# A hybrid decoder step on one core: the second layer's normalised operand is multiplied out ahead of the K/V evacuations, and the sample queries' copies are issued on ScalarE

## The chip, the cores and the metric

The kernel runs on one core of one Trainium2 chip. The metric is the device time of one execution in microseconds (us). The kernel before takes 1169.92 us, the median of three runs (1169.79 to 1174.06). Engines are named as in the profile: PE is TensorE, DVE VectorE, ACT ScalarE, POOL GpSimd, SP SyncE, which issues the DMAs.

## The reference

One step of a two-layer decoder of width 1024 runs on 512 prompt tokens and on 8 samples of 8 tokens each, 576 tokens in all. Layer 1 is a gated linear recurrence (HGRN2). Then one shared K/V is projected from its output, and layer 2 is sliding-window attention with a learned sink per head, over that K/V and, for the samples, over cached rows:

```python
hp, sp = hgrn2_layer(hp, s_zero, w_in_a, w_out_a, norm_a, onorm_a, lb)     # prompt
hs, ss = hgrn2_layer(hs, state_hgrn, w_in_a, w_out_a, norm_a, onorm_a, lb) # samples
kv_p, kv_s = shared_kv(hp, norm_kv, w_kv), shared_kv(hs, norm_kv, w_kv)    # rms_norm(x, g) @ w
q, gate = split(rms_norm(x, norm_b) @ w_in_b)
s = where(window_mask, q @ k.T * 64 ** -0.5, -inf)
p = softmax(concatenate([s, sink]))[..., :-1]
x = x + ((p @ v) * silu(gate)) @ w_out_b
y = rms_norm(x, norm_f)
```

Layer 2 has 32 query heads of 64 columns in 4 groups, each with one K/V head. The window is 128 tokens. All is float32.

## The kernel before

**Arithmetic.** Every float32 operand of a large product is split in two fp32r tiles: hi is a cast, lo is what the cast lost. A product is three passes over the contraction, w_hi·x_hi, w_hi·x_lo, w_lo·x_hi (`product_cols`, matmuls on L211). The weights come by DMA as "raw" and are split in `split_weights`: hi by ACT's cast (L200), lo by a subtraction (L204). Which engine subtracts is set by `share`: during the K/V projection DVE takes a quarter and POOL three quarters, in layer 2 POOL takes all (1024 columns in one instruction).

**Stages.** Layer 1 goes on to about 690 us, the K/V projection from there to about 718 us, its turning and the first queries to about 742, the attention to about 1142, the output projection's end, the final norm and the stores to the end. Tokens are worked on as columns, in two halves j of HN = 288. The hidden state is `hT` (128 partitions x 8 tiles k x 576), the normalised operand that the products read is `xhi`, `xlo` of the same shape.

**The layer boundary.** The K/V projection is run in two pairs of products: c0 = 0 makes K, c0 = 2 makes V. It reads the hidden state times its own norm's gain from `xhi`, `xlo`, made at the end of layer 1; each product `pkv` is 24 matmuls of 288 columns into a bank of PSUM, evacuated by DVE into `kf` with the factor 1/rms (the tile `rall`, `rts[j]` in the code; L1030). For K, ACT casts `KDh` (L1048), DVE subtracts `KDl` (L1051). For V, PE transposes `kf` into `pvw` (L1062), from which `Vc` is taken. Only when the V products of a half j have been computed may `xhi`, `xlo` of that half be overwritten with layer 2's operand. That is what `scaled` does (L515 to 521), for each k of a half: DVE multiplies `hT` by the gain and 1/rms into a tile u (288 columns, tag "nu", four buffers; L519), ACT casts it to `xhi` (L520), and POOL for even k, DVE for odd k subtracts into `xlo` (L521). With four buffers, the product for k + 4 waits until u of k has been subtracted.

**Layer 2.** `queries` makes the queries of two heads at a time: a product into a bank `pbq`, from which ACT casts QS (L1286), DVE subtracts into the other half of QS (L1289) and, where the bank holds the 64 sample tokens' queries too (j = 1), DVE copies these into `Qs` in two instructions of 64 columns (L1294). `attend_sample` runs the samples' scores `scs` on `Qs` (L1205, 1206). The prompt's attention goes through scores, softmax (`P`), transposition (`ph`, `pl`, `pk`), the product with V (`pav`, `low`) and the gate into `sgt`; `split_out` splits sgt into `ohb` (ACT, L1394) and `olb` (DVE, L1395), `sample_part` does the same for the samples' 64 columns (`ohb` L1266, `olb` L1267), and `out_halves` runs the output product `po` on them, added to hT on L1334. All these tiles lie in the pool `ab`; in it P, ph, pl and sgt have two buffers each.

**What sets the order.** The parts of layer 2 are interleaved by a written order and a pace per step (`ORDER`, `PACE`), and the tile scheduler then orders each engine's instructions by priority: code under `tc.high_priority(offset=BOOST)` (800) or `early(EARLYB)` (100) is put that far ahead of its place in the program. Each engine then executes its list in order. A tile that is read and written by several engines is guarded by semaphores. PSUM banks for the products are in rotation: three for `pkv`, `pbq`, `pbg` and `po` together, five for the rest.

Of the kernel before, what the change touches and what calls it, by code (L numbers as in the profile page):

```python
# [10 lines left out]
F32 = mybir.dt.float32  # L11
# [5 lines left out]
ALU = mybir.AluOpType  # L17
PSUM = bass.MemoryType.PSUM

P = 128  # L20
D = 1024
KT = D // P
# [5 lines left out]
HN = T // 2  # L28
# [55 lines left out]
def yoco_kernel(  # L84
# [26 lines left out]
    act, dve, pool, pe, sp = nc.scalar, nc.vector, nc.gpsimd, nc.tensor, nc.sync  # L111
# [20 lines left out]
    def half(name):  # L132
        return ps["m"].tile([P, 512], F32, tag="m", name=name)
# [50 lines left out]
    def vec(name, i):  # L184
        r, _ = vcol[name]
        return vT[:, r + i : r + i + 1]

    hT = res.tile([P, KT, T], F32, name="hT")
# [6 lines left out]
    def split_weights(src, name, parts=None):  # L195
        n = src.shape[1] * src.shape[2]
        raw = wts.tile([P, 1024], F32, tag="raw", name=f"raw_{name}", bufs=3)
        sp.dma_start(raw[:, :n].rearrange("p (a c) -> p a c", a=src.shape[1]), src)
        hi, lo = parts or [wts.tile([P, 1024], F32R, tag=t, name=f"{t}_{name}") for t in ("whi", "wlo")]
        act.copy(hi[:, :n], raw[:, :n])  # L200
        c = n * share[0] // 8
        for eng, r in ((dve, slice(0, c)), (pool, slice(c, n))):
            if r.start < r.stop:
                eng.tensor_tensor(lo[:, r], raw[:, r], hi[:, r].bitcast(F32), ALU.subtract)  # L204
        return hi, lo
# [13 lines left out]
    def product_half(pm, whi, wlo, x, j, width=P, w0=0, nk=KT):  # L219
        product_cols(pm, whi, wlo, x, j * HN, (j + 1) * HN, width, w0, nk)  # L220
# [42 lines left out]
    rts = [rall[:, j * HN : (j + 1) * HN] for j in range(2)]  # L263
# [248 lines left out]
        act.activation(rt, pss[:, :HN], AF.Ln, bias=eps_c, scale=1.0 / D)  # L512
        act.activation(rt, rt, AF.Exp, scale=-0.5)

    def scaled(rt, gname, one, j):  # L515
        r = slice(j * HN, (j + 1) * HN)
        for k in range(KT):
            u = one(f"u_{gname}{k}_{j}")
            dve.scalar_tensor_tensor(u, hT[:, k, r], vec(gname, k), rt, ALU.mult, ALU.mult)  # L519
            act.copy(xhi[:, k, r], u)  # L520
            (dve if k % 2 else pool).tensor_tensor(xlo[:, k, r], u, xhi[:, k, r].bitcast(F32), ALU.subtract)  # L521

# [3 lines left out]
    with ExitStack() as actx:  # L526
# [12 lines left out]
        for i in range(2):  # L539
            t = per.tile([P, T], F32, name=f"Xl{i}")  # L540
            dve.memset(t, 0.0)
            Xs.append(t)
            t = per.tile([P, DB, 16], F32, name=f"Qz{i}")
            dve.memset(t, 0.0)
            Qz.append(t)
            t = per.tile([P, P], F32, name=f"atts{i}")
            dve.memset(t, 0.0)
            att_s.append(t)
            t = per.tile([P, P], F32, name=f"vs{i}")
# [407 lines left out]
        for h in range(NH):  # L957
            nxt, chunks, n = {}, [], 0
# [21 lines left out]
    with ExitStack() as bctx:  # L980
# [33 lines left out]
        ab = bctx.enter_context(tc.tile_pool(name="ab", bufs=1))  # L1014
        with tc.tile_pool(name="kvx", bufs=1) as kvx:
            kvo = kvx.tile([P, 512], F32, name="kvo")
            kvs = kvx.tile([LS, 512], F32, name="kvs")
            kvw = [w_kv[:, c * P : (c + 1) * P].rearrange("(k p) c -> p k c", p=P) for c in range(4)]
            kfs = []
            for c0 in range(0, 4, 2):  # L1020
                ws = [split_weights(kvw[c], f"kv{c}") for c in (c0, c0 + 1)]
                kf = [kvx.tile([P, T], F32, tag=f"kf{c % 2}", name=f"kf{c}", bufs=2) for c in (c0, c0 + 1)]
                for j in range(2):
                    for c in range(2):
                        pm = half(f"pkv{c0 + c}_{j}")
                        product_half(pm, *ws[c], bx, j)
                        if c0 == 0 and c == 0:
                            with tc.high_priority(offset=BOOST):
                                feature_norm(j)
                        dve.tensor_tensor(kf[c][:, j * HN : (j + 1) * HN], pm[:, :HN], rts[j], ALU.mult)  # L1030
                    if c0:
                        with tc.high_priority(offset=BOOST):
                            scaled(
                                rts[j],
                                "norm_b",
                                lambda n: kvx.tile([P, HN], F32, tag="nu", name=n, bufs=4),
                                j,
                            )
                kfs += kf
            for c in range(4):  # L1040
                kf = kfs[c]
                if c < 2:
                    for gi in range(2):
                        g = 2 * c + gi
                        r0 = slice(64 * gi, 64 * gi + 64)
                        for s in range(2):
                            o0 = slice(64 * s, 64 * s + 64)
                            act.copy(KDh[o0, g, :], kf[r0, :LP])  # L1048
                        same, other = r0, slice(64 - 64 * gi, 128 - 64 * gi)
                        for o0 in (same, other):  # L1050
                            dve.tensor_tensor(KDl[o0, g, :], kf[r0, :LP], KDh[r0, g, :].bitcast(F32), ALU.subtract)  # L1051
                    act.copy(kS[:, c, :], kf[:, LP:])
                    pt = misc(f"pkw{c}")
                    pe.transpose(pt[:, :P], kf[:, LP - P : LP], ident)
                    pe.transpose(pt[:LS, P : 2 * P], kf[:, LP:], ident)
                    dve.tensor_copy(kvo[:, c * P : (c + 1) * P], pt[:, :P])
                    dve.tensor_copy(kvs[:, c * P : (c + 1) * P], pt[:LS, P : 2 * P])
                else:
                    g0 = 2 * (c - 2)
                    pt = misc(f"pvw{c}")  # L1060
                    for n in range(NC):
                        pe.transpose(pt[:, n * P : (n + 1) * P], kf[:, n * P : (n + 1) * P], ident)  # L1062
                    pt4 = pt.rearrange("p (n g d) -> p n g d", n=NC, g=2)
                    hi = Vc[:, :, g0 : g0 + 2, :64]
                    act.copy(hi, pt4)
                    dve.tensor_tensor(Vc[:, :, g0 : g0 + 2, 64:], pt4, hi.bitcast(F32), ALU.subtract)
                    dve.tensor_copy(kvo[:, c * P : (c + 1) * P], pt[:, 3 * P :])
                    pt2 = misc(f"pvs{c}")
                    pe.transpose(pt2[:LS, :P], kf[:, LP:], ident)
                    dve.tensor_copy(kvs[:, c * P : (c + 1) * P], pt2[:LS, :P])  # L1070
            dve.tensor_copy(vS[:LS, :], kvs[:, 256:])
            sp.dma_start(kvw_prompt[0].rearrange("s k g d -> s (k g d)"), kvo)
            for bb in range(DB):
                sp.dma_start(co[bb, P - DL :, :], kvs[bb * DL : (bb + 1) * DL, :])
# [194 lines left out]
        def queries(i, Qs, QS):  # L1269

            g, pp = i // 2, i % 2
            gr = slice(64 * (g % 2), 64 * (g % 2) + 64)
            hv = [slice(64 * par, 64 * par + 64) for par in range(2)]
            for pr in range(2):
                m = 2 * i + pr
                w = split_weights(w_in_b[0, :, m * P : (m + 1) * P].rearrange("(k p) c -> p k c", p=P), f"bq{m}")
                for j in range(2):
                    pm = half(f"pbq{m}_{j}")
                    c0, c1 = ((0, 256), (256, T))[j]
                    product_cols(pm, *w, bx, c0, c1)  # L1280
                    n = 256
                    Q = QS[pr][:, 4 * j : 4 * j + 4, :].rearrange("p b (a q) -> p a b q", a=2)
                    pq = pm[:, :n].rearrange("p (b q) -> p b q", b=4)
                    with early(EARLYB):
                        for par in range(2):
                            act.copy(Q[hv[par], par, :, :], pq[hv[par]])  # L1286
                        for par in range(2):
                            a, o = hv[par], hv[1 - par]
                            dve.tensor_tensor(  # L1289
                                Q[o, par, :, :], pq[a], Q[a, par, :, :].bitcast(F32), ALU.subtract  # L1290
                            )
                        if j == 1:
                            for par in range(2):
                                dve.tensor_copy(  # L1294
                                    Qs[gr, :, 4 * pp + 2 * pr + par, :],
                                    pm[hv[par], n : n + LS].rearrange("p (b i) -> p b i", i=8),
                                )
                    yield
# [142 lines left out]
        size = list(itertools.accumulate(8 if kind == "O" else 4 for kind, _ in order))  # L1441
# [131 lines left out]
```

## Time and profile before

| | |
|---|---|
| median of 3 runs | 1169.92 us (1169.79 to 1174.06) |
| profiled execution, its own time | 1169.39 us |
| its span in the trace | 1167.6 us |
| mean granted PE clock | 0.982 of full speed |
| PE busy | 1111.7 us, 95% |
| DVE busy | 895.4 us, 77% |
| ACT busy | 702.1 us, 60% |
| POOL busy | 340.7 us, 29% |

The profile is of one execution. Its span runs from the first recorded instruction to the last; the execution's own time is 1.8 us longer. A row of a timeline gives the start of a run of like instructions in us from the span's start, its duration, the engine, the line in the kernel, the operation with output and inputs, and in brackets the idle time of the engine before it with what ended it. Where a row ends in x4, its duration is that of four instructions. Windows give the busy time of each engine in a stretch and the clock that PE was granted there.

### The profile page before, as it was taken

To read this page: it belongs to the slowest core of one execution; us is meant where nothing else is said; L and a number is where in the kernel's file an instruction comes from. 1 tells how busy PE (TensorE), PEld (TensorE's weight loads), DVE (VectorE), ACT (ScalarE), POOL (GpSimd) and SP (SyncE) were. 2 spreads that over 40 slices of the span, in tenths; PEclk is the share of its full clock that TensorE was granted. 3 is DMA by queue.
4 is the path that set the end of the run, shared out by engine and by line. 5 is a ranking of instruction groups with operands and counts; after the bars stand their busy time and mean duration, and the time that the engine had idled before them with its cause. 6 is when DMAs were issued, how large, how long until landed. Compare 5 with 4: busy or idle time off the path is not lost.

```text
span 1167.6 us, 27339 instructions
## 1 busy us (share of the span) xinstructions
PE 1111.7 (95%) x10937; PEld 1078.1 (92%) x10937; DVE 895.4 (77%) x2090; ACT 702.1 (60%) x1700; POOL 340.7 (29%) x311
## 2 busy tenths in 40 slices
PE   5999999999999999999999987999999999999997
PEld 5999999999999999999999987989989999999986
DVE  8898776489984597893897779567787778777686
ACT  6776764466662567772767455557655764765545
POOL 1122221112121131110122155444543453454430
PEclk8999999999999999999999998989999999999999
DMA  5332233232332523332232332211212213112102
GB/s 154 100 112 86 84 109 112 59 110 76 110 117 66 147 74 113 97 107 74 76 111 77 103 91 74 68 55 56 73 39 71 74 55 91 56 55 73 56 19 82
DMA packets 161097, 98.01 MB, mean 84 GB/s; under 512 B 3897, under 2 KB 157546, under 8 KB 160938
## 3 DMA queue, kind: packets, MB, share of 16 engines
q1 hardware_dynamic: 160970, 96.26, 28.0%
q8 instruction: 86, 1.41, 0.5%
q14 instruction: 41, 0.34, 0.1%
HBM read 84.06 MB, written 14.16 MB: 84 GB/s over the span
## 4 chain that ended last, share of the span: by engine, by line
PE 45%; DVE 11%; ACT 6%; issue 2%; POOL 1%; DVEq 0%; ACTq 0%; POOLq 0%
PE pbg L211 7%; PE po L211 7%; PE pbq L211 5%; PE po L228 4%; PE pg L228 3%; PE pf L228 3%; PE pi L228 3%; PE pq L228 2%; PE pkv L211 2%; PE sc L1098 2%; ACT P L1127 1%; PE pav L1181 1%; PE pz L211 1%; DVE QS L1289 1%; PE pa L797 1%
## 5 line engine op out<-in xcount | busy, mean ns | idle before, releaser
L606 POOL TENSOR_TENSOR Xl<-Xl 128x72 f32<-128x72 f32 x80 | 50.3, 659 | 205.9 <-DVE Xl L603 204.7
L638 POOL TENSOR_TENSOR sg<-sg,lg 128x576 f32<-128x576 f32 x16 | 26.3, 1642 | 278.4 <-ACT lg L571 278.4
L200 ACT CAST whi_a<-raw_a 128x1024 fp32r<-128x1024 f32 x64 | 67.1, 1049 | 63.4 <-PE po L228 30.8
L204 DVE TENSOR_TENSOR wlo_a<-raw_a,whi_a 128x1024 fp32r<-128x1024 f32 x64 | 81.8, 1282 | 25.0 <-issue 23.6
L1127 ACT ACTIVATE P<-P,st 128x192 f32<-128x192 f32 (+2 forms) x128 | 54.1, 424 | 68.4 <-DVE st L1122 68.4
L1136 POOL TENSOR_SCALAR P<-P,st 128x192 f32<-128x192 f32 (+1 forms) x64 | 48.6, 769 | 117.9 <-DVE st L1129 99.4
L438 DVE TENSOR_TENSOR hT<-hT,po 128x576 f32<-128x576 f32 x32 | 24.1, 754 | 49.6 <-PE po L228 49.3
L200 ACT CAST whi_o<-raw_o 128x1024 fp32r<-128x1024 f32 x30 | 31.4, 1047 | 30.8 <-PE po L228 25.6
L204 POOL TENSOR_TENSOR wlo_bg<-raw_bg,whi_bg 128x1024 fp32r<-128x1024 f32 x16 | 38.4, 2402 | 35.5 <-ACT whi_bg L200 30.0
L228 PE MATMUL po<-oh,whi_o 128*128 128x288 f32 x256 | 42.8, 302 | 4.4 <-ACT whi_o L200 1.9
L211 PE MATMUL po<-olb,whi_o 128*128 128x288 f32 x224 | 43.0, 306 | 3.8 <-DVE olb L1395 1.9
L211 PE MATMUL po<-ohb,whi_o 128*128 128x288 f32 x224 | 43.6, 311 | 2.4 <-DVE Qs L1294 1.7
L662 POOL TENSOR_TENSOR vb<-vst,bmask 128x512 fp32r<-128x512 f32 x32 | 36.7, 1168 | 26.7 <-DVE vst L658 13.8
L204 POOL TENSOR_TENSOR wlo_bq<-raw_bq,whi_bq 128x1024 fp32r<-128x1024 f32 x16 | 38.8, 2430 | 19.2 <-ACT whi_bq L200 19.1
L228 PEld LDWEIGHTS po<-oh,whi_o 128*128 128x128 f32 x256 | 35.9, 188 | 6.3 <-ACT whi_o L200 2.2
L211 PE MATMUL pbq<-xhi,whi_bq 128*128 128x256 f32 (+1 forms) x256 | 41.4, 305 | 0.0
L211 PE MATMUL po<-ohb,wlo_o 128*128 128x288 f32 x224 | 41.3, 301 | 0.0
L228 PE MATMUL po<-ol,whi_o 128*128 128x288 f32 x256 | 40.5, 294 | 0.0
L211 PE MATMUL pbg<-xhi,whi_bg 128*128 128x288 f32 x256 | 40.5, 300 | 0.0
L228 PE MATMUL po<-oh,wlo_o 128*128 128x288 f32 x256 | 40.4, 294 | 0.0
L211 PE MATMUL pbg<-xhi,wlo_bg 128*128 128x288 f32 x256 | 40.1, 299 | 0.0
L204 POOL TENSOR_TENSOR wlo_o<-raw_o,whi_o 128x1024 fp32r<-128x1024 f32 x14 | 33.6, 2399 | 22.0 <-ACT whi_o L200 20.3
(385 smaller groups left out, 3761.4 us busy)
## 6 DMA issues: line engine op xcount, KB each, us to landing
raw_a<-in_w_in_a_dram SPq DMA_DIRECT2D x64, 512.0 KB
S<-in_state_hgrn_dram SPq DMA_DIRECT2D x32, 256.0 KB
out_dram<-S SPq DMA_DIRECT2D x32, 256.0 KB
raw_o<-in_w_out_a_dram SPq DMA_DIRECT2D x16, 512.0 KB
raw_bq<-in_w_in_b_dram SPq DMA_DIRECT2D x16, 512.0 KB
raw_bg<-in_w_in_b_dram SPq DMA_DIRECT2D x16, 512.0 KB
raw_o<-in_w_out_b_dram SPq DMA_DIRECT2D x16, 512.0 KB
xt<-in_x_prompt_dram SPq DMA_DIRECT2D x4, 512.0 KB
```

Source lines behind the costliest of these rows:

```text
L200: act.copy(hi[:, :n], raw[:, :n])
L204: eng.tensor_tensor(lo[:, r], raw[:, r], hi[:, r].bitcast(F32), ALU.subtract)
L211: pe.matmul(pm[:, : c1 - c0], w[:, k * width + w0 : k * width + w0 + P], x(k)[i][:, c0:c1], start=n == 0, stop=n == len(terms) - 1,)
L228: pe.matmul(pm[:, j, :HN], w[:, k * width + c0 : k * width + c0 + P], x(k, j), start=n == 0 and k == 0, stop=n == 2 and k == nk - 1,)
L438: dve.tensor_add(h2, h2, ps2(pm))
L606: pool.tensor_tensor(X8[:, :, j : j + 1], X8[:, :, j : j + 1], X8[:, :, k : k + 1], ALU.add)
L638: (pool if SGP else dve).tensor_tensor(sg, sg, l, ALU.mult)
L662: pool.tensor_tensor(t, view(vst.bitcast(F32), [[0, 4], [1, P]], off=half * P), view(bmask, [[1, 4], [0, P]]), ALU.mult,)
L797: pe.matmul(pa[32 * j : 32 * j + ns, c, t0 : t0 + nt], keys[:, c * P + s0 : c * P + s0 + ns], queries[:, c * P + t0 : c * P + t0 + nt], st ...
L1098: pe.matmul(sc[:, hf, k0[hf] :], QS[pr][:, 2 * n + hf, :], kk[:, g, ks], start=q == 0, stop=q == 1)
L1127: act.activation(x, x, AF.Exp, bias=st[:, a : a + 1], accum_out=st[:, 8 + a : 9 + a])
L1136: (pool if e == "p" else dve).tensor_scalar(x, x, st[:, 8 + a : 9 + a], None, ALU.mult)
```

## The change

Two things are changed. First, `scaled` makes only the products, into tiles that it is given, and a new function `operand` makes the cast and the subtraction. All 16 products are issued once, after the first pair of K/V products, into tiles that live until the operand is made: four of 288 columns in the old "nu" buffers, the others in the attention's buffers of P (two tiles of two products each), ph and pl (four tiles), and sgt (two tiles, four products). `operand` stands where `scaled` stood, after the second pair's evacuations of a half, with the same offset. Second, the two copies into `Qs` are issued on ACT in place of DVE.

```diff
--- before.py
+++ after.py
@@ -512,11 +512,16 @@
         act.activation(rt, pss[:, :HN], AF.Ln, bias=eps_c, scale=1.0 / D)
         act.activation(rt, rt, AF.Exp, scale=-0.5)
 
-    def scaled(rt, gname, one, j):
+    def scaled(us, gname, j):
+
         r = slice(j * HN, (j + 1) * HN)
-        for k in range(KT):
-            u = one(f"u_{gname}{k}_{j}")
-            dve.scalar_tensor_tensor(u, hT[:, k, r], vec(gname, k), rt, ALU.mult, ALU.mult)
+        for k, u in enumerate(us):
+            dve.scalar_tensor_tensor(u, hT[:, k, r], vec(gname, k), rts[j], ALU.mult, ALU.mult)
+
+    def operand(us, j):
+
+        r = slice(j * HN, (j + 1) * HN)
+        for k, u in enumerate(us):
             act.copy(xhi[:, k, r], u)
             (dve if k % 2 else pool).tensor_tensor(xlo[:, k, r], u, xhi[:, k, r].bitcast(F32), ALU.subtract)
 
@@ -1030,12 +1035,15 @@
                         dve.tensor_tensor(kf[c][:, j * HN : (j + 1) * HN], pm[:, :HN], rts[j], ALU.mult)
                     if c0:
                         with tc.high_priority(offset=BOOST):
-                            scaled(
-                                rts[j],
-                                "norm_b",
-                                lambda n: kvx.tile([P, HN], F32, tag="nu", name=n, bufs=4),
-                                j,
-                            )
+                            operand(us[j], j)
+                if not c0:
+
+                    us = [[kvx.tile([P, HN], F32, tag="nu", name=f"nu{k}", bufs=4) for k in range(4)], []]
+                    for n, (tag, size) in enumerate((("P", 2), ("P", 2), ("ph", 1), ("pl", 1), ("ph", 1), ("pl", 1), ("sgt", 3), ("sgt", 1))):
+                        t = ab.tile([P, size * HN], F32, tag=tag, name=f"us{n}", bufs=2)
+                        us[n > 1] += [t[:, i * HN : (i + 1) * HN] for i in range(size)]
+                    for i in range(2):
+                        scaled(us[i], "norm_b", i)
                 kfs += kf
             for c in range(4):
                 kf = kfs[c]
@@ -1291,7 +1299,7 @@
                             )
                         if j == 1:
                             for par in range(2):
-                                dve.tensor_copy(
+                                act.copy(
                                     Qs[gr, :, 4 * pp + 2 * pr + par, :],
                                     pm[hv[par], n : n + LS].rearrange("p (b i) -> p b i", i=8),
                                 )
```

How DVE's list at the layer boundary changes is shown by its rows from the place on where the first kf is evacuated (names are out<-inputs, the number behind a name is that of the tile, the last column partitions x elements; u_norm_b are the products in the kernel before). Before:

```order
L519 SCALAR_TENSOR_TENSOR u_norm_b_0_9516<-hT,vT,rall 128x288
L519 SCALAR_TENSOR_TENSOR u_norm_b_0_9520<-hT,vT,rall 128x288
L519 SCALAR_TENSOR_TENSOR u_norm_b_0_9524<-hT,vT,rall 128x288
L519 SCALAR_TENSOR_TENSOR u_norm_b_0_9528<-hT,vT,rall 128x288
L1030 TENSOR_TENSOR kf_9334<-pkv_0_9336,rall 128x288
L1030 TENSOR_TENSOR kf_9335<-pkv_0_9366,rall 128x288
L1030 TENSOR_TENSOR kf_9334<-pkv_1_9392,rall 128x288
L204 TENSOR_TENSOR wlo_kv_9451<-raw_kv_9448,whi_kv_9450 128x256
L1051 TENSOR_TENSOR KDl<-kf_9334,KDh 64x512 x3
```

After (nu and us are the products, L1035 and L1059 are the old L1030 and L1051):

```order
L1035 TENSOR_TENSOR kf_9334<-pkv_0_9336,rall 128x288
L519 SCALAR_TENSOR_TENSOR nu_9448<-hT,vT,rall 128x288
L519 SCALAR_TENSOR_TENSOR nu_9449<-hT,vT,rall 128x288
L519 SCALAR_TENSOR_TENSOR nu_9450<-hT,vT,rall 128x288
L519 SCALAR_TENSOR_TENSOR nu_9451<-hT,vT,rall 128x288
L519 SCALAR_TENSOR_TENSOR us_9452<-hT,vT,rall 128x288 x2
L519 SCALAR_TENSOR_TENSOR us_9453<-hT,vT,rall 128x288
L1035 TENSOR_TENSOR kf_9335<-pkv_0_9366,rall 128x288
L519 SCALAR_TENSOR_TENSOR us_9453<-hT,vT,rall 128x288
L519 SCALAR_TENSOR_TENSOR us_9454<-hT,vT,rall 128x288
L519 SCALAR_TENSOR_TENSOR us_9455<-hT,vT,rall 128x288
L519 SCALAR_TENSOR_TENSOR us_9456<-hT,vT,rall 128x288
```

The first evacuation now stands ahead of all products; the products, which stood four ahead of it and twelve behind the K operands, stand between the evacuations of the first pair.

The second place on DVE is the end of the boundary, ahead of the last two evacuations kf, the ones that PE's transposes `pvw` read. Before:

```order
L521 TENSOR_TENSOR xlo<-u_norm_b_0_9536,xhi 128x288
L519 SCALAR_TENSOR_TENSOR u_norm_b_1_9600<-hT,vT,rall 128x288
L519 SCALAR_TENSOR_TENSOR u_norm_b_1_9604<-hT,vT,rall 128x288
L519 SCALAR_TENSOR_TENSOR u_norm_b_1_9608<-hT,vT,rall 128x288
L521 TENSOR_TENSOR xlo<-u_norm_b_0_9544,xhi 128x288
L1030 TENSOR_TENSOR kf_9463<-pkv_0_9490,rall 128x288
L519 SCALAR_TENSOR_TENSOR u_norm_b_1_9612<-hT,vT,rall 128x288
L1030 TENSOR_TENSOR kf_9462<-pkv_1_9548,rall 128x288
L1030 TENSOR_TENSOR kf_9463<-pkv_1_9574,rall 128x288
```

After:

```order
L1035 TENSOR_TENSOR kf_9490<-pkv_0_9492,rall 128x288
L1059 TENSOR_TENSOR KDl<-kf_9335,KDh 64x512 x2
L526 TENSOR_TENSOR xlo<-nu_9449,xhi 128x288
L1035 TENSOR_TENSOR kf_9491<-pkv_0_9518,rall 128x288
L526 TENSOR_TENSOR xlo<-nu_9451,xhi 128x288
L526 TENSOR_TENSOR xlo<-us_9452,xhi 128x288
L526 TENSOR_TENSOR xlo<-us_9453,xhi 128x288
L1035 TENSOR_TENSOR kf_9490<-pkv_1_9560,rall 128x288
L1035 TENSOR_TENSOR kf_9491<-pkv_1_9586,rall 128x288
```

The four products that stood among the subtractions there are gone; four subtractions xlo stand in front of the last two kf where two stood.

On POOL the sequence of operations is the same at this place, and so are the orders on PE and of SP's DMAs. The third place is where a bank of queries with the samples' columns is taken up. DVE before, in the attention's unit whose olb of 64 columns follows:

```order
L1395 TENSOR_TENSOR olb_0_11234<-sgt_10324,ohb_0_11233 128x512
L1395 TENSOR_TENSOR olb_1_11240<-sgt_10324,ohb_1_11239 128x512
L1289 TENSOR_TENSOR QS_1_11046<-pbq_1_11250,QS_1_11046 64x4x64 x2
L1294 COPY Qs_9697<-pbq_1_11250 64x8x8 x2
L1267 TENSOR_TENSOR olb_1_11240<-oS_10816,ohb_1_11239 128x64
L1157 TENSOR_TENSOR pl_0_0_11288<-ptr_0_0_11281,ph_0_0_11287 128x256
L1164 TENSOR_TENSOR pk_0_0_11291<-ptm_0_0_11282,pk_0_0_11291 64x256
```

ACT after, with what each instruction waits for in brackets (the semaphore of an engine or of a DMA queue):

```order
L1402 CAST ohb_0_11229<-sgt_10320 128x512 [waits DVE_49]
L1402 CAST ohb_1_11235<-sgt_10320 128x512
L1274 CAST ohb_1_11235<-oS_10812 128x64
L1294 CAST QS_1_11042<-pbq_1_11246 64x4x64 [waits PE_49]
L1294 CAST QS_1_11042<-pbq_1_11246 64x4x64
L1164 CAST ph_0_0_11283<-ptr_0_0_11277 128x256 [waits PE_49]
L1169 CAST pk_0_0_11287<-ptm_0_0_11278 64x256 [waits PE_49]
L200 CAST whi_o_2_11410<-raw_o_2_11408 128x1024 [waits DMAHW3_49,Pool_49]
L1302 COPY Qs_9693<-pbq_1_11246 64x8x8 [waits DVE_49]
L1302 COPY Qs_9693<-pbq_1_11246 64x8x8
```

The two copies, which stood on DVE between its subtractions into QS and the olb subtraction of 64 columns, stand on ACT behind the casts of QS, ph, pk and a weight cast, and the first of the two waits for DVE.

## The prediction

> **What bounds the kernel now.** The page comes first: its span, its busy times and the chain that ended last.
>
> ```profile
> span 1167.6 us, 27339 instructions
> PE 1111.7 (95%) x10937; PEld 1078.1 (92%) x10937; DVE 895.4 (77%) x2090; ACT 702.1 (60%) x1700; POOL 340.7 (29%) x311
> PE 45%; DVE 11%; ACT 6%; issue 2%; POOL 1%; DVEq 0%; ACTq 0%; POOLq 0%
> ```
>
> TensorE (PE) is busy for 95% of the span. Another engine's saving counts only where PE waits for it, so I read the stretches in which PE waits. First the layer boundary, in the timelines of PE, DVE, POOL and ACT (start, duration, engine, line; in brackets the idle time before and its releaser).
>
> ```profile
> 718.06 0.38 PE L1062 MATMUL pvw<-ident,kf 128*128 128x128 f32 x2
> 724.78 0.69 PE L1062 MATMUL pvw<-ident,kf 128*128 128x128 f32 x2 [6.33 <-DVE kf L1030]
> ```
> ```profile
> 695.68 1.81 DVE L519 SCALAR_TENSOR_TENSOR u_norm_b<-hT,vT,rall 128x288 f32<-128x288 f32 x4 [2.39 <-ACT rall L513]
> 706.18 0.46 DVE L1030 TENSOR_TENSOR kf<-pkv,rall 128x288 f32<-128x288 f32 x1
> 708.31 2.81 DVE L1051 TENSOR_TENSOR KDl<-kf,KDh 64x512 fp32r<-64x512 f32 x4
> 716.30 6.12 DVE L519 SCALAR_TENSOR_TENSOR u_norm_b<-hT,vT,rall 128x288 f32<-128x288 f32 x3
> 724.28 0.81 DVE L1030 TENSOR_TENSOR kf<-pkv,rall 128x288 f32<-128x288 f32 x2
> 727.86 1.06 DVE L521 TENSOR_TENSOR xlo<-u_norm_b,xhi 128x288 fp32r<-128x288 f32 x1
> ```
> ```profile
> 702.01 1.84 POOL L204 TENSOR_TENSOR wlo_kv<-raw_kv,whi_kv 128x768 fp32r<-128x768 f32 x1 [6.85 <-ACT whi_kv L200]
> 717.13 4.98 POOL L204 TENSOR_TENSOR wlo_bq<-raw_bq,whi_bq 128x1024 fp32r<-128x1024 f32 x2
> 727.56 2.01 POOL L521 TENSOR_TENSOR xlo<-u_norm_b,xhi 128x288 fp32r<-128x288 f32 x2 [3.52 <-ACT xhi L520]
> ```
>
> PE runs dry at 718.44 and waits 6.33 us for the last kf evacuations, which stand on DVE behind three products that take 6.12 us; four took 1.81 us at 695.68. The slow three lie under POOL's two L204 subtractions: a DVE instruction with two SBUF inputs does not run while a POOL subtraction runs, and one slips through between two of POOL's. Afterwards the clock is about halved (the windows view; busy us of PE, PEld, DVE, ACT, POOL, then the granted PE clock, DMA share and GB/s; two later places are shown with it):
>
> ```profile
> 724.00:730.00 6.00, 5.22 (x26) 5.15 (x27) 6.00 (x15) 2.93 (x7) 2.05 (x3) 0.54 0.26 77
> 856.00:860.00 4.00, 4.00 (x21) 4.00 (x21) 2.46 (x13) 1.96 (x9) 0.00 (x0) 0.59 0.42 121
> 960.00:964.00 4.00, 2.97 (x14) 3.00 (x15) 3.84 (x10) 1.34 (x4) 2.28 (x1) 0.71 0.14 33
> 964.00:968.00 4.00, 4.00 (x29) 4.00 (x29) 2.43 (x13) 1.92 (x10) 0.00 (x0) 0.87 0.29 102
> ```
>
> Then the attention, 726 to 1142 us, in the view of waits (total, times, longest):
>
> ```profile
> PE scs L1205 <- DVE Qs L1294: 5.0, 2, 2.8
> PE po L211 <- DVE olb L1267: 1.8, 1, 1.8
> PE po L211 <- DVE Qs L1294: 1.7, 1, 1.7
> ```
>
> **Part 1, the operand.** No instruction is added; 16 products move ahead. Sixteen at 0.45 us (1.81/4) are 7.2 us; 12 of them leave the stretch behind 712 us and go into DVE's idle time behind 696 us. If their place were the whole matter, kf would come as soon as PE ends and the wait would go: 6.3 us and the half-clocked start behind it. Against this stands POOL, whose row has not changed.
>
> From the rows: DVE starts at 695.68 with kf, then 13 products and two more kf at about 0.45 each, and meets POOL's L204 at 702.01. The last three products wait for its end at 703.85 and finish near 705.2. DVE's share of the next split ends at 705.6, when POOL's second L204 is due (its cast now stands behind three KDh casts instead of four). One KDl gets in (2.81/4, 0.7 us), the next waits about 1.84 us, and kf1 of the second half comes near 708.8 where it came at 706.18. The matmuls whose operands pass here need them at 707.01 and 710.17 (the third passes of the next two products):
>
> ```profile
> 707.01 1.21 PE L211 MATMUL pkv<-xhi,wlo_kv 128*128 128x288 f32 x8
> 710.17 1.21 PE L211 MATMUL pkv<-xhi,wlo_kv 128*128 128x288 f32 x8
> 706.67 2.53 ACT L1048 CAST KDh<-kf 64x512 fp32r<-64x512 f32 x4 [0.46 <-DVE kf L1030]
> 710.50 1.44 ACT L520 CAST xhi<-u_norm_b 128x288 fp32r<-128x288 f32 x4 [1.04 <-PE pkv L211]
> ```
>
> DVE's parts are ready near 705.6 and 709.5: hidden under PE's passes, the second with 0.7 us to spare; past that PE would wait as long as it is late. But ACT's four KDh follow kf1 (2.53 us, to 711.7), and the eight xhi casts then run through without a wait: 711.9 to 714.8 at 0.36 each (1.44/4). POOL's four xlo start near 712.4; so does DVE's last but one KDl. From there they alternate (727.56 and 727.86 above: a pair takes about 1.05 us), four POOL xlo against KDl, KDl, xlo, xlo on DVE, until about 717.2. Then POOL has its two L204 (4.98 us), and DVE's two remaining xlo stand in front of the last two kf: one slips in between, one follows near 722.5. kf comes at 723.2 and PE goes on near 723.3: **1.5 us** won. The bounds: 6.2 us if DVE is through before POOL's L204, about 3.9 if one more DVE instruction gets in ahead (the tie at 712.4 is 0.1 us wide by these rows), 0 if POOL is as late as before. I take 1.5 because the alternation is what the rows show. Of the slow clock behind it (5.22 us busy at 0.54 up to 730: 2.4 lost) an earlier start in the same slow stretch saves little: 0.5, between 0 and 2.4.
>
> The attention's buffers are free for this: the products are read to the end by about 727, and P, the first of them that is wanted, is written behind 742 (some 1.5 us earlier now). Only products that live 13 us longer would make the scores wait.
>
> ```profile
> 742.97 0.22 DVE L1102 CUSTOM_DVE_ANT_0 P<-sc,amask 128x64 f32<-128x64 f32 x1
> ```
>
> **Part 2, the copies.** 32 copies of 0.22 us leave DVE; ACT's nearest row is kS (0.24).
>
> ```profile
> L1294 DVE COPY Qs<-pbq x32: 216/222/229, 736.1 to 1067.9; 64x64 f32<-64x64 f32 x32
> L1052 ACT COPY kS<-kf x2: 238/242/245, 706.0 to 709.2; 128x64 f32<-128x64 f32 x2
> ```
>
> The order shows that they do not simply run behind ACT's casts: each pair waits for DVE, and what DVE last has to do with that bank is its subtraction. So nothing is won where PE waits for Qs itself. At 777 and 1068:
>
> ```profile
> 776.26 0.86 DVE L1289 TENSOR_TENSOR QS<-pbq,QS 64x256 fp32r<-64x256 f32 x2
> 777.13 0.46 DVE L1294 COPY Qs<-pbq 64x64 f32<-64x64 f32 x2
> 777.64 0.70 PE L1205 MATMUL scs<-kcT,Qs 128*64 128x128 f32 x4 [2.85 <-DVE Qs L1294]
> ```
>
> DVE ends the subtraction at 777.12 either way; two copies and one more hand-over on ACT give 777.7: 0.1 us lost, twice. The wait put behind it on ACT delays low, ph and pk casts by up to 0.9 us, which DVE and then PE need; I price that at 0.5 in all, between 0 and the rival below. If the wait were not there, the copies would run beside the subtraction (0.86) and be done before it: 1.3 us of the wait at 777 would go. The Trainium skill (PSUM — Partial Sum Buffer, section "PSUM bank collisions raise a hardware error") asks that a bank be guarded as a whole between engines, two readers included. By that rule the wait stays; the order has it, and no run here shows the chip without it.
>
> What is won lies behind the copies on DVE:
>
> ```profile
> 849.49 0.24 ACT L1266 CAST ohb<-oS 128x64 fp32r<-128x64 f32 x1
> 851.82 0.46 DVE L1294 COPY Qs<-pbq 64x64 f32<-64x64 f32 x2
> 852.29 2.33 DVE L1267 TENSOR_TENSOR olb<-oS,ohb 128x64 fp32r<-128x64 f32 x1
> 852.19 2.35 POOL L204 TENSOR_TENSOR wlo_o<-raw_o,whi_o 128x1024 fp32r<-128x1024 f32 x1 [0.72 <-ACT whi_o L200]
> 854.67 0.40 PE L211 MATMUL po<-olb,whi_o 128*128 128x288 f32 x1 [1.83 <-DVE olb L1267]
> 949.80 0.46 DVE L1294 COPY Qs<-pbq 64x64 f32<-64x64 f32 x2
> 950.27 2.39 DVE L1267 TENSOR_TENSOR olb<-oS,ohb 128x64 fp32r<-128x64 f32 x1
> 950.17 2.41 POOL L204 TENSOR_TENSOR wlo_o<-raw_o,whi_o 128x1024 fp32r<-128x1024 f32 x1 [0.71 <-ACT whi_o L200]
> 961.03 0.78 PE L211 MATMUL po<-ohb,whi_o 128*128 128x288 f32 x4 [1.71 <-DVE Qs L1294]
> ```
>
> A 64-column subtraction takes 2.3 us twice, since POOL's L204 begins 0.10 us ahead of it. Without the copies it starts at 851.82 and 949.80, 0.37 us ahead of POOL, and is done; its cast is there since 849.73. At 854 this takes 1.83 us from PE and the slow clock that follows (0.59 over 4 us: 1.6), together **3.4**. At 950 DVE gains 2.3 us on its way to the subtraction that frees a bank at 961: of the 1.71 us I take off 1.5 (ACT now copies behind low, ph and half of pk, which costs 0.2), and its slow clock (4 us at 0.71 and 4 at 0.87: 1.7): **3.2**. Bounds for each pair: 0 if POOL still comes first, and the full sum.
>
> The 0.59 stands right behind a gap of 1.83 us, the 0.71 behind one of 1.71 us. The Trainium skill (TensorE: Matmul & The Clock Gate, section "Why this matters for your kernels") holds that only idle gaps beyond about 3 us bring the slow clock back; the trace says otherwise. By that rule the two places would be worth 3.3 us less.
>
> **Sum.** 1.5 + 0.5 + 3.4 + 3.2 - 0.2 - 0.5 = 7.9 us off the profiled execution's 1169.39 (span 1167.6 and 1.8 around it; the median of the runs, 1169.92, is 0.5 above): **1161.5 us**.
>
> **Rivals.**
> - *The boundary opens wholly*: DVE passes POOL before its L204, kf follows PE at once. 6.2 + 2.4 in place of 2.0: 6.6 more, 1154.9. For it: the tie at 712.4; against it: the alternation. Chance 0.17.
> - *POOL keeps its lead*: earlier DVE work moves ACT's casts and POOL forward too, the short subtractions are caught as before. 6.6 less: 1168.1. For it: the margin is only 0.37 us. Against it: ACT's casts that release POOL's L204 do not pass the copies, and the subtractions do. Chance 0.26.
> - *The slow clock is not the gaps'*: the stretches behind 856 and 961 stay slow though the gaps go, 3.3 less: 1164.8. The rows speak against it, since each stretch begins within 1.2 us of a gap's end. Chance 0.04. (This is how the Trainium skill's rule on gaps, named above, would have it.)
> - *ACT becomes the late engine*: a pair of copies holds ACT for DVE's subtraction and its own time, 0.86 + 0.46 = 1.3 us, with softmax casts queued behind. With 12 of the 16 pairs reaching PE it costs 15.6, against 2.0 won at the boundary and nothing at the two collisions: 1183.0; it decides from 2 of 16 on, and passes 0.5% from 6 (7.8 - 2.0 = 5.8). Against it: ACT is at 60% and mostly waits itself. Chance 0.08.
>
> **How the numbers follow.** The forecast case has 0.45 and its own range of 1158 to 1164.5. The range of 8 in 10 takes in the first two rivals: 1154.5 to 1168.5. About 0.5% (5.8 us, below 1164.1) is what a measurement can tell from none. Faster: 0.41 of the forecast, 0.17 and 0.03 of the second rival, 0.61. Same: 0.04, 0.23, 0.04, and 0.02 of the last, 0.33. Slower: 0.06.
>
> **What would show it.** In the changed profile: products back to back from 696 us; PE's wait for pvw near 4.9 us instead of 6.33, with two xlo of DVE stretched by POOL's L204 in front of kf; olb subtractions of about 0.1 us near 850 and 944; waits for Qs on ACT's line, about as long as DVE's were. A pvw wait under 2 us would refute the first term, a 2.3 us olb the second and third, growing waits of PE on ph, pk or low the small price of ACT.

## The result, and the profile after

The changed kernel takes 1159.82 us (median of 4 runs, 1159.44 to 1161.31); the kernel before, run beside it, 1170.79 us (median of 4, 1169.79 to 1174.06). The ratio is 0.9907, with a 95% interval of 0.9892 to 0.9922: 0.9% faster. The forecast was 1161.5 us, in a range of 1154.5 to 1168.5. The profiled execution took 1159.44 us, 9.95 us less than the one of before.

The page of the changed kernel, first lines:

```profile
span 1157.6 us, 27335 instructions
PE 1107.2 (96%) x10937; PEld 1073.8 (93%) x10937; DVE 884.8 (76%) x2058; ACT 707.8 (61%) x1732; POOL 339.9 (29%) x311
```

DVE has 10.6 us less to do and ACT 5.7 us more, but the span is read at PE: 10.0 us shorter, of which PE's busy time gives 4.5 (the same matmuls at a mean granted clock of 0.988 against 0.982) and its idle time the rest.

The layer boundary, in the timelines of PE, DVE and POOL (start, duration, engine, line; idle time before and its releaser in brackets). L1035, L1059, L1070 and L526 are the old L1030, L1051, L1062 and L521:

```profile
718.51 0.38 PE L1070 MATMUL pvw<-ident,kf 128*128 128x128 f32 x2
722.44 0.44 PE L1070 MATMUL pvw<-ident,kf 128*128 128x128 f32 x2 [3.54 <-DVE kf L1035]
724.07 2.06 PE L211 MATMUL pbq<-xhi,whi_bq 128*128 128x256 f32 x8
725.92 1.22 PE L211 MATMUL pbq<-xlo,whi_bq 128*128 128x256 f32 x8
727.93 1.34 PE L211 MATMUL pbq<-xhi,whi_bq 128*128 128x320 f32 x8
```
```profile
705.72 2.93 DVE L1059 TENSOR_TENSOR KDl<-kf,KDh 64x512 fp32r<-64x512 f32 x2
708.68 0.46 DVE L1035 TENSOR_TENSOR kf<-pkv,rall 128x288 f32<-128x288 f32 x1
715.87 0.45 DVE L1035 TENSOR_TENSOR kf<-pkv,rall 128x288 f32<-128x288 f32 x1
716.24 0.69 DVE L526 TENSOR_TENSOR xlo<-nu,xhi 128x288 fp32r<-128x288 f32 x1
716.85 5.16 DVE L526 TENSOR_TENSOR xlo<-us,xhi 128x288 fp32r<-128x288 f32 x2
721.94 0.81 DVE L1035 TENSOR_TENSOR kf<-pkv,rall 128x288 f32<-128x288 f32 x2
```
```profile
712.38 2.03 POOL L526 TENSOR_TENSOR xlo<-nu,xhi 128x288 fp32r<-128x288 f32 x2 [4.28 <-ACT xhi L525]
714.38 2.24 POOL L526 TENSOR_TENSOR xlo<-us,xhi 128x288 fp32r<-128x288 f32 x2
716.57 5.12 POOL L204 TENSOR_TENSOR wlo_bq<-raw_bq,whi_bq 128x1024 fp32r<-128x1024 f32 x2
```

The last two kf still stand behind two DVE subtractions that take 5.16 us, and these lie almost exactly (716.85 to 722.01) under POOL's two weight subtractions (716.57 to 721.69). PE waits 3.54 us where it waited 6.33.

The two collisions, DVE and POOL of the changed kernel:

```profile
848.40 0.23 DVE L1275 TENSOR_TENSOR olb<-oS,ohb 128x64 fp32r<-128x64 f32 x1
942.85 0.23 DVE L1275 TENSOR_TENSOR olb<-oS,ohb 128x64 fp32r<-128x64 f32 x1
```
```profile
848.75 2.39 POOL L204 TENSOR_TENSOR wlo_o<-raw_o,whi_o 128x1024 fp32r<-128x1024 f32 x1 [0.73 <-ACT whi_o L200]
943.20 2.40 POOL L204 TENSOR_TENSOR wlo_o<-raw_o,whi_o 128x1024 fp32r<-128x1024 f32 x1 [0.71 <-ACT whi_o L200]
```

Both olb subtractions of 64 columns start 0.35 us ahead of POOL and take 0.23 us instead of 2.33 and 2.39. PE's rows there have no gap left, and the windows behind them show the full clock (after the busy times, the granted clock):

```profile
849.00:853.00 4.00, 4.00 (x33) 4.00 (x32) 3.21 (x15) 1.38 (x7) 2.15 (x1) 1.00 0.10 23
950.00:954.00 4.00, 4.00 (x33) 4.00 (x32) 3.52 (x9) 2.41 (x7) 3.09 (x2) 1.00 0.00 0
954.00:958.00 4.00, 4.00 (x33) 4.00 (x32) 2.65 (x13) 1.72 (x8) 0.00 (x0) 1.00 0.42 137
```

Where the copies now stand, PE waits as long as before, only on another engine (waits of PE; and the group of the copies with what ACT waits for ahead of them):

```profile
PE scs L1213 <- ACT Qs L1302: 4.8, 2, 2.8
```
```profile
L1302 ACT COPY Qs<-pbq x32: 203/207/212, 733.3 to 1057.6; 64x64 f32<-64x64 f32 x32
  DVE QS L1297: 9.5, 9
```

Both profiles hold the same 10,937 matmuls, so that the lag of one trace on the other can be read at the start of the same matmul. The step between two rows is what the place between them gave:

| matmul | before | after | lag | step | what lies between |
|---|---|---|---|---|---|
| first two pvw | 718.06 | 718.51 | +0.45 | | ahead of the change's first gain |
| last pvw behind the gap | 724.78 | 722.44 | -2.34 | -2.79 | the wait for kf |
| second bank of pbq | 730.73 | 727.93 | -2.80 | -0.46 | its slow clock |
| po at the first olb | 849.64 | 846.20 | -3.44 | -0.64 | scs near 777 and small changes |
| po behind the first olb | 854.91 | 849.37 | -5.54 | -2.10 | the gap at 854 |
| po, some 4 us later | 859.28 | 852.22 | -7.06 | -1.52 | its slow clock |
| po behind 961 | 964.97 | 954.67 | -10.30 | -3.24 | the gap at 961 and its slow clock |
| last matmul | | | -9.98 | +0.32 | the rest |

### The profile page after: what moved, and what is told of

The parts are those of the page before. It is cut to its first block, busy times and chain, and to the rows that moved or that the text cites. A ratio compares the mean times of both kernels' runs of the same rounds, so it can differ in the third digit from the quotient of the medians.

```text
span 1157.6 us, 27335 instructions
## 1 busy us (share of the span) xinstructions
PE 1107.2 (96%) x10937; PEld 1073.8 (93%) x10937; DVE 884.8 (76%) x2058; ACT 707.8 (61%) x1732; POOL 339.9 (29%) x311
## 4 chain that ended last, share of the span: by engine, by line
PE 47%; DVE 10%; ACT 4%; issue 1%; POOL 0%; DVEq 0%; ACTq 0%
PE pbg L211 8%; PE pbq L211 6%; PE po L211 6%; PE po L228 4%; PE pg L228 3%; PE pf L228 3%; PE pi L228 3%; PE pq L228 2%; PE sc L1106 2%; PE pav L1189 1%; PE pkv L211 1%; PE pz L211 1%; PE pa L802 1%; PE ptr L1157 1%; ACT P L1135 1%
## 5 line engine op out<-in xcount | busy, mean ns | idle before, releaser
L1297 DVE TENSOR_TENSOR QS<-pbq,QS 64x256 fp32r<-64x256 f32 x64 | 27.0, 422 | 17.9 <-ACT QS L1294 17.2
```

What stands on the lines that cost most here:

```text
L1297: dve.tensor_tensor(Q[o, par, :, :], pq[a], Q[a, par, :, :].bitcast(F32), ALU.subtract)
```

## The experiments

Times are medians beside runs of the kernel before on the same chip; the ratio is to that kernel, with its 95% interval. The kernel before took 1171.34 us (9 runs) beside the first three kernels below and the one with the boundary's POOL subtractions on DVE, and 1171.63 us (15 runs) beside the other four.

**The operand alone.** The copies into Qs are put back on DVE:

```diff
-                                act.copy(
+                                dve.tensor_copy(
                                     Qs[gr, :, 4 * pp + 2 * pr + par, :],
```

> The operand's part alone: the copies into Qs are back on DVE, all else is the changed kernel. Theory A (two separate gains, each at its place): the wait of PE for kf is about 3.5 us as in the changed kernel (6.33 before), the two 64-column olb subtractions near 849 and 947 stay at 2.3 us, PE's gaps of 1.8 and 1.7 us stay with the slow clock behind them; 3.4 us less than before, a ratio near 0.997. Theory B (one gain: the work arriving 3 us earlier by itself moves DVE and POOL apart at the two later places): the olb subtractions are short here too, 10 us less, a ratio near 0.991.

Measured: 1166.71 us, ratio 0.9963 (0.9951 to 0.9976). The waits of PE and DVE's subtractions at the two later places:

```profile
PE pvw L1070 <- DVE kf L1035: 3.6, 1, 3.6
PE po L211 <- DVE olb L1275: 1.9, 1, 1.9
PE po L211 <- DVE Qs L1302: 1.7, 1, 1.7
```
```profile
849.99 2.34 DVE L1275 TENSOR_TENSOR olb<-oS,ohb 128x64 fp32r<-128x64 f32 x1
947.92 2.40 DVE L1275 TENSOR_TENSOR olb<-oS,ohb 128x64 fp32r<-128x64 f32 x1
```

The wait for kf is the changed kernel's, the collisions and the gaps of PE that come of them are all there. Theory A holds, theory B falls: an earlier start of the attention does not move DVE and POOL apart.

**The copies alone.** The kernel before with this edit:

```diff
-                                dve.tensor_copy(
+                                act.copy(
                                     Qs[gr, :, 4 * pp + 2 * pr + par, :],
```

> The copies' part alone: the copies into Qs on ACT, the products made as before. Theory A: the wait for kf stays at 6.3 us with its slow clock; the two olb subtractions start ahead of POOL's subtraction and take 0.1 to 0.25 us; PE's gaps near 854 and 961 and the slow clock behind them go; about 7.0 us less than before, a ratio near 0.994. Theory B: without the earlier start of the attention the olb subtractions are caught as before: 0 to 0.5 us, a ratio of 0.9995 to 1.

Measured: 1164.04 us, ratio 0.9945 (0.9932 to 0.9958). PE waits 6.3 us for kf as before; the olb subtractions are short:

```profile
PE pvw L1062 <- DVE kf L1030: 6.3, 1, 6.3
```
```profile
855.82 0.23 DVE L1267 TENSOR_TENSOR olb<-oS,ohb 128x64 fp32r<-128x64 f32 x1
950.65 0.22 DVE L1267 TENSOR_TENSOR olb<-oS,ohb 128x64 fp32r<-128x64 f32 x1
```

Theory A holds again. The parts add up: 0.37% and 0.55% give 0.92%, together they gave 0.93%.

**The collision without the copies.** The kernel before, DVE with all its 32 copies, but the 64-column olb subtractions put ahead in DVE's list:

```diff
             act.copy(oh[:, LP:], new[g][:, m, :])
-            dve.tensor_tensor(ol[:, LP:], new[g][:, m, :], oh[:, LP:].bitcast(F32), ALU.subtract)
+            with early(2 * EARLYB if g < 3 else 0):
+                dve.tensor_tensor(ol[:, LP:], new[g][:, m, :], oh[:, LP:].bitcast(F32), ALU.subtract)
```

> The kernel before, with one thing changed: the 64-column olb subtractions of the first three groups have a higher priority, so that DVE runs them ahead of the QS subtractions and the copies into Qs. DVE has all its 32 copies. Theory A (the gain was the collision with POOL's weight subtraction, not DVE's load): both olb subtractions take 0.25 us or less, the gaps of PE near 854 and 961 go with their slow clock, about 7 us less, a ratio near 0.994. Theory C (the gain was the 7.1 us of copies taken off DVE): nothing, a ratio of 0.999 to 1.001.

Measured: 1165.65 us, ratio 0.9947 (0.9933 to 0.9960). DVE and POOL at the first place:

```profile
852.83 0.21 DVE L1268 TENSOR_TENSOR olb<-oS,ohb 128x64 fp32r<-128x64 f32 x1
```
```profile
854.80 2.38 POOL L204 TENSOR_TENSOR wlo_o<-raw_o,whi_o 128x1024 fp32r<-128x1024 f32 x1 [1.21 <-ACT whi_o L200]
```

At the second place it is the same: the subtraction starts at 948.18, takes 0.21 us, and POOL's begins at 950.14. PE has neither of the two gaps, and the clock is full in both places. Nearly the whole gain of the copies is had without moving one of them. Theory C falls: it was the order of two instructions against POOL's, not the 7.1 us of work that DVE lost.

**One more copy on DVE, short and wide.** The changed kernel, with a copy that nobody needs behind the QS subtraction; the first of the two kernels has this edit, the second takes 256 columns (`pm[hv[par], :256]`):

```diff
                             for par in range(2):
+                                dve.tensor_copy(spare, pm[hv[par], n : n + LS]) if par < 1 else None
                                 act.copy(
                                     Qs[gr, :, 4 * pp + 2 * pr + par, :],
```

> The changed kernel with one more DVE copy per bank of samples' queries, 64x64 out of the bank into a tile that nobody reads (0.22 us, 16 of them, 3.6 us of DVE), right behind the subtraction into QS and so ahead of the 64-column olb subtraction. In the changed kernel olb starts 0.35 us ahead of POOL's weight subtraction. Theory A (a collision with a threshold): olb still starts 0.1 us ahead, takes 0.25 us, and the time is 0 to 1 us above the changed kernel (the copies on ACT wait 0.2 us longer), a ratio near 0.991. Theory C (DVE's load): half of the 7 us comes back, 1163 to 1164, a ratio near 0.994.

> As the kernel with one small copy, but the copy has 256 columns (0.3 to 0.45 us, 16 of them, 5 to 7 us of DVE). Theory A: with 0.35 us or more in front of it olb starts at or behind POOL's start and is caught, 2.3 us, at both places; PE's gaps of 1.8 and 1.7 us are back with their slow clock, about 7 us above the changed kernel, near 1167, a ratio near 0.9965; if the copy is shorter than 0.35 us it is as with the small copy. Theory C: in proportion to the small copy, 1165 to 1167 if that one took 1163 to 1164.

Measured: 1162.11 us with the short copy, ratio 0.9913 (0.9882 to 0.9944); 1167.60 us with the wide one, ratio 0.9970 (0.9951 to 0.9989). DVE and POOL at both places, first with the short copy:

```profile
850.38 0.23 DVE L1275 TENSOR_TENSOR olb<-oS,ohb 128x64 fp32r<-128x64 f32 x1
944.90 0.22 DVE L1275 TENSOR_TENSOR olb<-oS,ohb 128x64 fp32r<-128x64 f32 x1
```
```profile
850.51 2.40 POOL L204 TENSOR_TENSOR wlo_o<-raw_o,whi_o 128x1024 fp32r<-128x1024 f32 x1 [0.73 <-ACT whi_o L200]
945.03 2.41 POOL L204 TENSOR_TENSOR wlo_o<-raw_o,whi_o 128x1024 fp32r<-128x1024 f32 x1 [0.71 <-ACT whi_o L200]
```

Then with the wide one:

```profile
847.55 2.35 DVE L1275 TENSOR_TENSOR olb<-oS,ohb 128x64 fp32r<-128x64 f32 x1
944.42 2.41 DVE L1275 TENSOR_TENSOR olb<-oS,ohb 128x64 fp32r<-128x64 f32 x1
```
```profile
847.48 2.35 POOL L204 TENSOR_TENSOR wlo_o<-raw_o,whi_o 128x1024 fp32r<-128x1024 f32 x1 [0.72 <-ACT whi_o L200]
944.35 2.40 POOL L204 TENSOR_TENSOR wlo_o<-raw_o,whi_o 128x1024 fp32r<-128x1024 f32 x1 [0.71 <-ACT whi_o L200]
```

Here theory A's threshold shows most plainly. If it starts 0.13 us ahead of POOL the subtraction takes 0.23 us, and 0.07 us behind POOL's start it takes 2.35: a copy that is 0.20 us longer (0.42 against 0.22) makes the subtraction 2.1 to 2.2 us longer at each place. By the ratios the short copy stands 0.7 us above the changed kernel and the wide one 7.4 (0.0006 and 0.0063 of 1171), where theory A had 0 to 1 and 7, and a load would give the short copy half of what it gives the wide one. The intervals are wide: the short copy's four runs lie between 1157.55 and 1164.98, so that the times alone would not decide; the rows do. Two things did not come as theory A had it. The profiled execution with the wide copy, at 1164.26 us the fastest of ten, has PE's gaps but no slow clock behind them; the last section comes back to this. And not all of its time is the collision's: the wide copy also holds up the copies into Qs, and PE's second wait for scs is 2.68 us instead of 1.95.

**The boundary's POOL subtractions.** The changed kernel with the low parts of the first two query weights made on DVE:

```diff
             for pr in range(2):
                 m = 2 * i + pr
+                share[0] = 8 if m < 2 else LO_B
                 w = split_weights(w_in_b[0, :, m * P : (m + 1) * P].rearrange("(k p) c -> p k c", p=P), f"bq{m}")
...
         def gates(i, sgS, sgt):
+            share[0] = LO_B
```

> The changed kernel, with the low parts of the first two query weights subtracted on DVE (1.28 us each by the rows of that form) and not on POOL, so that POOL has no 1024-column subtraction between 716 and 722 us. Theory A (DVE's xlo subtractions and with them kf are held by POOL's two weight subtractions): the two xlo ahead of kf take 0.9 us and not 5.2, PE's wait for kf falls from 3.5 to under 1 us, the slow clock behind it goes; 3 to 4.5 us less than the changed kernel, about 1156, a ratio near 0.987. Theory D (kf is late for another reason: ACT's xhi casts, or DVE simply has too much in front of it): the wait stays above 3 us, and the kernel is 0 to 2 us slower than the changed one for the second weight's subtraction in front of QS.

Measured: 1155.60 us, ratio 0.9866 (0.9852 to 0.9879). DVE, then PE at the boundary, then the window behind it with the granted clock:

```profile
718.71 0.81 DVE L526 TENSOR_TENSOR xlo<-us,xhi 128x288 fp32r<-128x288 f32 x2
719.45 0.45 DVE L1035 TENSOR_TENSOR kf<-pkv,rall 128x288 f32<-128x288 f32 x1
719.82 1.21 DVE L204 TENSOR_TENSOR wlo_bq<-raw_bq,whi_bq 128x1024 fp32r<-128x1024 f32 x1
720.95 0.45 DVE L1035 TENSOR_TENSOR kf<-pkv,rall 128x288 f32<-128x288 f32 x1
```
```profile
721.45 0.44 PE L1070 MATMUL pvw<-ident,kf 128*128 128x128 f32 x2 [0.16 <-DVE kf L1035]
```
```profile
722.00:728.00 6.00, 5.75 (x44) 5.75 (x45) 5.92 (x16) 2.71 (x8) 4.89 (x7) 1.00 0.42 128
```

The same two xlo subtractions take 0.81 us instead of 5.16, PE waits 0.16 us instead of 3.54, and the clock stays full. By the ratios this is 4.8 us below the changed kernel, a little more than the 3 to 4.5 expected. Theory A holds; theory D falls. That DVE does the two subtractions in 1.21 us each, where POOL took 2.56 (5.12/2), costs nothing that shows.

**The copies ahead of the subtraction.** The changed kernel with the loops of the copies and of DVE's subtractions in the other order:

```diff
                         for par in range(2):
                             act.copy(Q[hv[par], par, :, :], pq[hv[par]])
+                        if j == 1:
+                            for par in range(2):
+                                act.copy(
...
                         for par in range(2):
                             a, o = hv[par], hv[1 - par]
                             dve.tensor_tensor(
                                 Q[o, par, :, :], pq[a], Q[a, par, :, :].bitcast(F32), ALU.subtract
                             )
-                        if j == 1:
...
```

> The changed kernel with the two copies into Qs issued ahead of DVE's subtraction out of the same bank, so that DVE waits for ACT and not ACT for DVE. Theory A (the Qs copies' wait for DVE is what PE's waits for scs consist of): the copies end about 0.45 us after ACT's QS casts; PE's wait for scs falls from 2.81 to about 1.6 us near 775 and from 1.95 to about 1.1 us near 1058, and the slow clock behind the first (up to 3.4 us) shrinks or goes; DVE's subtractions start up to 0.46 us later, mostly hidden; 2 to 5 us less than the changed kernel, about 1156, a ratio near 0.987. Rival (DVE's subtractions are the ones that PE needs): the waits move to sc and po, and the time is that of the changed kernel or 1 to 2 us above it, a ratio of 0.990 to 0.993.

Measured: 1159.34 us, ratio 0.9896 (0.9878 to 0.9915), against 0.9907 (0.9892 to 0.9922) of the changed kernel: not told apart. ACT's copies and PE's scores near 773:

```profile
771.89 0.75 ACT L1294 CAST QS<-pbq 64x256 fp32r<-64x256 f32 x2
772.65 0.43 ACT L1297 COPY Qs<-pbq 64x64 f32<-64x64 f32 x2
```
```profile
773.13 0.45 PE L1213 MATMUL scs<-kcT,Qs 128*64 128x128 f32 x4 [2.35 <-ACT Qs L1297]
774.95 2.23 PE L211 MATMUL pbg<-xlo,whi_bg 128*128 128x288 f32 x8
```

The mechanism is as expected, the size is not. The copies come right behind ACT's casts, and the scores start 1.56 us earlier than in the changed kernel (774.69), 0.2 of which this trace brought along. But the scheduler put seven gate matmuls that had filled the wait there (pbg<-xlo) behind the scores, so the wait fell only by 0.46 us. The slow stretch behind it is one of 3.41 us instead of two, as expected. Near 1056 the wait fell from 1.95 to 1.22 us, but PE then waits 0.52 us on sc for DVE's pl at 1077, where the changed kernel does not, and its lead over the changed kernel goes from 2.23 back to 1.55 us: the rival's shift of the waits is there, and small. The profiled execution is 1.4 us shorter, the median 0.5 us (1.3 by the ratios): less than the 2 to 5 us that theory A gave.

**Both edits together.** The last two edits on the changed kernel.

> Two edits together on the changed kernel: the first two query weights' low parts on DVE, and the copies into Qs ahead of DVE's subtraction. Theory A (the places are apart, the gains add up): 4 us from the first and 2 to 5 from the second, 1151 to 1154, a ratio of 0.983 to 0.985. Rival (the second edit delays DVE's subtractions where PE needs them): 1155 to 1157.

Measured: 1153.13 us (1152.32 to 1158.38, 5 runs), ratio 0.9849 (0.9827 to 0.9870). It has the lowest median of the study, 0.6% below the changed kernel by the ratios. Theory A's range was 1151 to 1154 us, the rival's 1155 to 1157; the interval reaches from the one into the other. Most of the gain is the boundary's edit; what the second one adds to it lies within the intervals (0.9866 alone).

## Why the prediction was right

**The bound.** PE was the place to read from. All steps of the table above 1 us lie at waits of PE that the prediction had named, or at the slow clock behind them.

**The operand: mechanism right, size too small.** The prediction said that kf would still be held by POOL's two weight subtractions, with two xlo in front of it, one slipping in between and one following. That is what the trace shows, and the kernel with the weight subtractions on DVE confirms it. The step that was mis-sized is the alternation of POOL's and DVE's subtractions ahead of them: 1.5 us forecast, 2.79 measured. The prediction let the second half's first kf come near 708.8 and POOL's four xlo end near 717.2; with the 0.45 us by which this trace lags there, 709.3 and 717.7. Measured are 708.68 and 716.62. One cause is in the rows: DVE began the two KDl ahead of that kf at 705.72 and not at 706.05 (705.6 and the lag), and they took 2.93 us and not 3.2, so that kf, and with it ACT's casts and POOL's first xlo, came some 0.5 us sooner. The other is the sum itself: four pairs of 1.05 us from 712.4 on end at 716.6, not at 717.2. Of this 1.1 us, POOL's two weight subtractions took back 0.14 (5.12 against 4.98), and the way from their end to PE's next matmul was 0.4 us shorter than forecast (0.75 against 1.1), which together makes the 1.3 us by which the term was too small. The slow clock gave 0.46 us against 0.5.

**The copies: right in place and size.** At 854, 3.4 us were forecast and 2.10 + 1.52 = 3.6 measured; at 961, 3.2 and 3.24. At 961 two errors cancel: the gap gave 1.8 us (the lag is -8.86 right behind it) against 1.5, the slow clock 1.44 against 1.7, which was priced over 4 us of the first window though PE was busy for only 2.97 of them. There is luck in the slow clock too: both terms, 3.3 of the 7.9 us, were read from one execution, and in another kernel's profile the same kind of gap has none behind it (last section). The reason was right: the kernel with the olb subtraction put ahead wins nearly as much with DVE's load unchanged. The margin in front of POOL is 0.35 us against 0.37 forecast, and the rival that had POOL keep its lead (0.26) turned on just that margin, which an added copy of 0.42 us uses up.

**The price of ACT: put too high, and small.** 0.7 us were put on the copies' hand-over and on casts queued behind them. The scores' wait near 777 is 2.81 us against 2.85 and near 1068 1.95 against 2.20. ACT does stand 9.5 us, in nine waits, for DVE's subtraction ahead of its copies, but no new wait of PE shows for it. Of the rest of the table, 0.64 us were won and 0.32 lost, the latter in one wait of PE for hT near 1106 (0.83 us instead of 0.53); which of these small steps are ACT's is not shown. So the sum of 7.9 us became 10.4 from the boundary on (9.98 in all, since this trace lagged by 0.45 there): 1.3 more from the alternation, 1.0 from this term and the small steps together, 0.2 from the collisions.

**The rule of the Trainium skill on gaps** (TensorE: Matmul & The Clock Gate, section "Why this matters for your kernels") would have made the two places worth 3.3 us less. The trace differs from it: a slow stretch stood behind gaps of 1.83 and 1.71 us and is gone with them, 1.52 us of the table at the first place alone. What it may have hung on is told in the last section.

## What to carry to other kernels

Look for short instructions that take ten times their usual time, and for what runs on the neighbouring engine then: here a DVE subtraction of 64 columns cost PE 1.8 us and more because POOL's long one began 0.1 us ahead of it, and any edit that puts the short one first wins that. Then look whether PE waits for the short one. In the kernel before two more of these subtractions are caught, near 922 and 1020 us, and PE has no wait for either; one near 1010 us is still caught in the changed kernel and costs nothing that shows. A forecast of such a place is a matter of tenths of a microsecond, so give the start times of both engines and the margin between them. The same holds at a boundary: moving DVE's work out of the stretch in which DVE is on the path gave 0.37% alone, and taking the two long POOL subtractions away from it gave another 0.41% on top. No run took them away with DVE's work in its old place, so it is open whether that alone would have been enough.

## What the runs showed of the hardware

**What a POOL subtraction holds up.** The DVE instructions that were held in these rows (products, xlo, olb) take all their operands from SBUF. The evacuation kf, which reads one SBUF tile and a bank of PSUM, was not held: in the kernel before one starts at 706.18, 0.03 us behind a POOL subtraction of 1.85 us, and takes its usual 0.46 us, while DVE's next instruction, a weight subtraction of 256 columns, takes 1.73 us instead of 0.42 and ends 0.28 us behind POOL's.

**A short gap alone does not bring the slow clock.** In the kernel with the wide copy PE has its gaps back, and the clock stays at 1.00 behind two of them:

```profile
849.96 0.40 PE L211 MATMUL po<-olb,whi_o 128*128 128x288 f32 x1 [1.83 <-DVE olb L1275]
955.93 0.80 PE L211 MATMUL po<-ohb,whi_o 128*128 128x288 f32 x4 [2.45 <-ACT Qs L1302]
```
```profile
850.00:854.00 4.00, 4.00 (x31) 4.00 (x32) 3.34 (x15) 1.09 (x6) 0.00 (x0) 1.00 0.47 133
956.00:960.00 4.00, 4.00 (x31) 4.00 (x32) 3.86 (x15) 0.00 (x0) 0.32 (x1) 1.00 0.43 133
```

A gap of 1.83 us was followed by 0.59 in the kernel before and by 1.00 here; 1.71 us by 0.71 there, and 2.45 us by 1.00 here. In the traces' clock records the slow stretches begin at multiples of 3.41 us from each other (in the kernel before 722.7, 777.3, 855.8, 961.7), and from the layer boundary to the end of the attention the stretch of 3.41 us ahead of each of these is idle by half or more of it, by the matmuls' rows (0.54 at 852.4, 0.50 at 958.2), while at 1064.1, where a gap of 2.20 us is cut by the edge, it is idle by 0.44 and nothing follows. The reading that fits best is a fixed grid on which a gap counts by its share of one cell. The edge at a half is not sharp: in the same profile a cell idle by 0.45 (302.9) is followed by a slow one, in the wide copy's one of 0.39 (773.7), and with the operand alone one of 0.55 (1062.2) is not. No run here shifted the grid on purpose, so this stays a reading. It would be one source of the scatter between executions of one kernel: the ten with the wide copy go from 1164.26 us at a mean granted clock of 0.985 to 1174.04 us at 0.977. And it would mean that the 1.5 us or so of slow clock behind a short gap are won in some executions and not in others.
